# First pieces from the raw input, its squares in the second pass, zero matmuls ahead of the first product, another order of passes in each feed-forward and five early down tiles

## The chip, the cores and the metric

The kernel runs on one core of a Trainium2 chip, in one launch. The metric is the device time of that launch in microseconds (us). The engines are named as in the profile: PE (matrix products), PEld (its weight loads), DVE (vector), ACT (scalar), POOL (GpSimd) and SP (which here only issues DMAs). Each engine runs its instructions in the order of the program; they wait for each other and for DMAs on semaphores.

## The reference

A two-layer decoder trunk over 512 positions of width 2048, in float32. Each layer is a half feed-forward, a mixer and a half feed-forward, so there are four feed-forwards; only they and the last norm are touched by the change.

```python
def rms_norm(x, g):
    y = x32 * lax.rsqrt(jnp.mean(x32 * x32, axis=-1, keepdims=True) + NORM_EPS)
    return y * g

def swiglu(x, w_gate, w_up, w_down):
    return (jax.nn.silu(x @ w_gate) * (x @ w_up)) @ w_down      # 2048 -> 1536 -> 2048

for i in range(DEPTH):                                          # DEPTH = 2
    h = h + 0.5 * swiglu(rms_norm(h, norm_g[i, 0]), ffn_w_gate[i, 0], ffn_w_up[i, 0], ffn_w_down[i, 0])
    h = h + mixer(rms_norm(h, norm_g[i, 1]))                    # even_mixer or odd_mixer
    h = h + 0.5 * swiglu(rms_norm(h, norm_g[i, 2]), ffn_w_gate[i, 1], ffn_w_up[i, 1], ffn_w_down[i, 1])
return rms_norm(h, final_norm)
```

## The kernel before, in words

Activations lie transposed, 16 blocks of 128 channels by 512 positions. A product keeps float32 accuracy by splitting both factors into a high and a low part: `mm3` (lines 289 to 292) issues three matmuls, high by high, high by low, low by high.

**Weights.** `plan_and_uses` lists every weight tile in the order of use. SP loads them into nine `raw` buffers (line 246). `split_to` makes the high part `wh` on ACT (261) and the low part `wl` on DVE (262), and, for tiles that stand in `sums`, adds or subtracts two raw tiles on DVE (266). `take` keeps the splits seven tiles ahead of the one in use (`NSPL`): a split is issued in the engines' queues just before the matmuls of the tile seven ahead of it in use have their turn.

**A feed-forward's products.** Gate and up projections are formed by a scheme of seven products in place of eight, over halves of the input (`Pieces`: two input blocks give B11, B21, B22, T1 to T4). The 1536 hidden columns are three units of 512. For each unit `three` does three products (B11, B21, T4: 24 tiles, 144 matmuls, six PSUM banks) and `four` does four (T1, T3, T2, B22: 32 tiles, 192 matmuls, eight banks); a tile is 6 matmuls. The order is line 56:

```python
PASSES = ((0, 0), (1, 0), (0, 1), (2, 0), (1, 1), (2, 1))      # (unit, is it `four`)
```

B11, B21, B22 and T4 come from `Pieces.early` (486 to 500), T1 to T3 from `Pieces.late` (502 to 515), one pair of blocks at a time. Small work is laid between the tiles by generators: after each tile of `three`, `beside()` is called once and runs a generator to its next `yield`. In the first pass of the first feed-forward that generator is `first_pieces` (890 to 906): for each pair it scales the two input blocks by the gain on ACT (`xb`, 895), forms differences on DVE (490), splits (300, 301), and squares both blocks on ACT (372). In the second pass it is `then_late` (587 to 592): `late`, and after it the norm's reduction `ng`.

**The norm.** `Norm.add` (370 to 380) squares a block on ACT; from the third square on, GpSimd adds it with an accumulating DMA into one of two sums (378), and each such DMA waits on GpSimd for the one before it on the same sum. `Norm.stages` (382 to 392) reduces both sums over channels with 16 one-column matmuls on PE (`nps`, 387).

**After `four`.** `to_hidden` (548 to 577) forms the hidden unit: adds on DVE (549), two silus for each of two row halves on ACT (553, 557), four multiplications on DVE (565), then four times four transposes on PE (575) with a split each. It is a generator of 17 yields; the first transposes come at its 14th step. Unit 0's steps are run by the ticks of the fourth pass, the others in the last two `four` passes and among the down products.

**Down products.** The first `FIRST` = 4 output tiles keep a PSUM bank each (line 651) and are fed from the hidden units one after the other, 12 matmuls per tile and unit; the other tiles are done whole. In the last feed-forward `last` (1091 to 1100) scales the output blocks by the norm: of each eight pairs three on GpSimd, five on DVE.

Of the kernel before, what the change touches and what calls it, by code (L numbers as in the profile page):

```python
# [11 lines left out]
F32R = mybir.dt.float32r  # L12
# [37 lines left out]
NRAW = 9  # L50
NSPL = 7
# [4 lines left out]
PASSES = ((0, 0), (1, 0), (0, 1), (2, 0), (1, 1), (2, 1))  # L56

FIRST = 4
# [13 lines left out]
def plan_and_uses():  # L72
# [15 lines left out]
    def ffn_products(i, j, down):  # L88


        for u, four in PASSES:
# [26 lines left out]
    ffn_products(0, 0, PAIR_DOWN)  # L118
# [86 lines left out]
def trunk(ctx: ExitStack, tc: tile.TileContext, xT, pos_row, pos_col, wts, gains, consts, bias_a_in, bias_b_in, outT):  # L205
# [131 lines left out]
    nc.scalar.dma_start(gn, gains)  # L337
    for k in range(HK):
# [136 lines left out]
    class Pieces:  # L475
# [25 lines left out]

        def late(self):
# [19 lines left out]
    def ffn_products(pieces, norm, resid_in, sink, down, feed=None, beside=()):  # L522
# [25 lines left out]
        def to_hidden(u, c11, u2, s4, s5, s7, c12):  # L548
# [21 lines left out]
            yield  # L570
# [8 lines left out]
        def ahead_pieces():  # L579
            for k in range(HK):  # L580
                for e in range(k + 1, min(k + 4, HK)):
                    pieces.get(e, "B11", False)
                yield
                yield
                yield

        def then_late():
            for _ in range(HK):
                next(late, None)
                yield  # L590
                yield
            yield from ng
# [21 lines left out]
        def four(u):  # L614
# [3 lines left out]
            for k in range(HK):  # L618
# [3 lines left out]
                if k % 2:  # L622
                    tick()
# [6 lines left out]
                if k % 2:  # L630
                    tick()
# [3 lines left out]
            side.append(turned[u])  # L635

        feed = ahead_pieces() if feed is None else feed
        rest = then_late()
        for u, is_four in PASSES:
            if is_four:  # L640
                four(u)
            elif u == 0:
                three(u, lambda: next(feed, None))
                finish(feed)
            elif u == 1:
                three(u, lambda: next(rest, None))
                finish(rest)
# [10 lines left out]
        finish(turned[2])  # L658
        for pd, job in zip(pds, down):
            down_half(pd, job, hid, 4)  # L660
            down_done(pd, job, resid_in, sink)
# [227 lines left out]

    def first_pieces():  # L890
        for k in range(HK):
            bs = []
            for d in (k, HK + k):
                b = blk("xb")
                nc.scalar.activation(b, xs[d], AF.Copy, scale=g_norm(0)(d))
                bs.append(b)
            in0.add(k, *bs)
            del bs, b
            next(in0.work[k])
            yield  # L900
# [275 lines left out]
```

## Time and profile before

| | us |
|---|---|
| median of 3 timed runs | 2268.35 |
| lowest, highest | 2267.42, 2269.26 |
| the profiled execution, its time | 2269.59 |
| its span, first to last instruction | 2267.8 |
| PE busy in that span | 2218.3 |

The profiled execution's granted clock is 0.995 on average. About 1.8 us of its time lies outside the span. The page of the profile gives busy times, the span in 40 slices, the chain that ended last and the costliest groups of instructions; the trace behind it was asked for waits, stretches, single lines and instructions in order of time. A row `a <- b: t` of the waits reads: a stood idle t us until b was done.

### The profile page before, as it was taken

What the parts mean: (1) busy time and instruction counts of PE and PEld (TensorE: products, weight loads), DVE (VectorE), ACT (ScalarE), POOL (GpSimd) and SP (SyncE); (2) the same over time, 40 slices, a digit from 0 to 9 for tenths busy, and PEclk for the clock granted to TensorE, in tenths of its full rate; (3) what the DMA queues carried; (4) which work ended last, traced back from release to release, by engine and by line L of the source; (5) the groups of instructions that cost most, each with busy time, mean ns of one, the idle gap of its engine ahead of it and who ended that gap; (6) DMA issues with size and microseconds to landing.
All of it is one profiled execution on the core that took longest, in us unless ns stands there. A gap on an engine that the chain in (4) does not pass through costs nothing.

```text
span 2267.8 us, 30596 instructions
## 1 busy us (share of the span) xinstructions
PE 2218.3 (98%) x10272; PEld 1853.0 (82%) x10272; DVE 1570.6 (69%) x2694; ACT 1111.5 (49%) x2002; POOL 159.0 (7%) x190
## 2 busy tenths in 40 slices
PE   7999999999999999999999999999999999999997
PEld 5878788989888888878788878788888888878787
DVE  7979865464645578798646889855335677889734
ACT  8655444333334476555445554443235566554443
POOL 2000011000001020000010000011200010000013
PEclk9999999999999999999999999999999999999998
DMA  9756554423223396566577666554332377656444
GB/s 298 210 171 186 155 180 146 123 66 93 86 76 112 110 274 185 174 195 180 168 194 196 187 177 185 148 187 150 100 98 71 118 220 227 186 173 177 152 135 144
DMA packets 207981, 363.70 MB, mean 160 GB/s; under 512 B 23120, under 2 KB 46032, under 8 KB 207824
## 3 DMA queue, kind: packets, MB, share of 16 engines
q1 hardware_dynamic: 173552, 299.77, 44.6%
q10 hardware_dynamic: 26208, 47.30, 6.4%
q0 software_dynamic: 8064, 14.68, 3.8%
q8 instruction: 80, 1.31, 0.2%
q14 instruction: 77, 0.63, 0.1%
HBM read 321.82 MB, written 25.17 MB: 153 GB/s over the span
## 4 chain that ended last, share of the span: by engine, by line
PE 92%; DVE 3%; ACT 1%; issue 1%; DMA 0%; POOL 0%; DVEq 0%; ACTq 0%; POOLq 0%
PE pb L291 8%; PE pb L290 8%; PE pb L292 8%; PE pd L291 7%; PE pd L292 7%; PE pd L290 7%; PE pa L290 5%; PE pa L292 5%; PE pa L291 5%; PE pj L290 5%; PE pj L292 5%; PE pj L291 5%; PE wo L290 3%; PE wo L292 3%; PE wo L291 3%; PE pr L290 2%
## 5 line engine op out<-in xcount | busy, mean ns | idle before, releaser
L262 DVE TENSOR_TENSOR wl<-raw,wh 128x512 fp32r<-128x512 f32 (+3 forms) x1159 | 780.3, 686 | 465.2 <-ACT wh L261 442.4
L261 ACT ACTIVATE wh<-raw 128x512 fp32r<-128x512 f32 (+3 forms) x1159 | 689.6, 610 | 627.6 <-DVE wl L262 130.9
L290 PE MATMUL pd<-hidh,wh 128*128 128x512 f32 (+1 forms) x816 | 308.3, 378 | 2.9 <-ACT hidh L300 2.9
L291 PE MATMUL pd<-hidl,wh 128*128 128x512 f32 (+1 forms) x816 | 308.2, 378 | 1.4 <-DVE hidl L301 1.4
L292 PE MATMUL pd<-hidh,wl 128*128 128x512 f32 (+1 forms) x816 | 307.4, 377 | 0.0
L266 DVE TENSOR_TENSOR raw<-raw,raw 128x512 f32<-128x512 f32 x384 | 262.4, 683 | 0.0
L290 PE MATMUL pa<-wh,pbh 128*128 128x512 f32 x576 | 230.0, 399 | 16.0 <-ACT pbh L300 13.1
L291 PE MATMUL pa<-wl,pbh 128*128 128x512 f32 x576 | 227.6, 395 | 0.3
L292 PE MATMUL pa<-wh,pbl 128*128 128x512 f32 x576 | 227.5, 395 | 0.0
L290 PE MATMUL pj<-xgh,wh 128*128 128x512 f32 x464 | 181.7, 392 | 0.0
L292 PE MATMUL pj<-xgh,wl 128*128 128x512 f32 x464 | 180.8, 390 | 0.0
L291 PE MATMUL pj<-xgl,wh 128*128 128x512 f32 x464 | 180.7, 389 | 0.0
L290 PEld LDWEIGHTS pd<-hidh,wh 128*128 128x128 f32 x816 | 153.5, 188 | 31.7 <-ACT hidh L300 3.8
L291 PEld LDWEIGHTS pd<-hidl,wh 128*128 128x128 f32 x816 | 153.5, 188 | 31.5 <-DVE hidl L301 3.4
L292 PEld LDWEIGHTS pd<-hidh,wl 128*128 128x128 f32 x816 | 153.6, 188 | 27.6
L292 PE MATMUL pb<-wh,ptl 128*128 128x512 f32 x384 | 149.4, 389 | 0.0
L291 PE MATMUL pb<-wl,pth 128*128 128x512 f32 x384 | 149.4, 389 | 0.0
L290 PE MATMUL pb<-wh,pth 128*128 128x512 f32 x384 | 149.4, 389 | 0.0
L290 PEld LDWEIGHTS pa<-wh,pbh 128*128 128x128 f32 x576 | 110.2, 191 | 40.2 <-ACT pbh L300 14.8
L380 POOL TENSOR_TENSOR sq<-sq,sq 128x512 f32<-128x512 f32 (+1 forms) x50 | 61.8, 1237 | 1015.1 <-ACT sq L372 802.4
L292 PEld LDWEIGHTS pa<-wh,pbl 128*128 128x128 f32 x576 | 109.8, 191 | 25.0 <-DVE pbl L301 1.9
L291 PEld LDWEIGHTS pa<-wl,pbh 128*128 128x128 f32 x576 | 109.9, 191 | 24.1 <-DVE wl L262 2.0
(239 smaller groups left out, 3551.6 us busy)
## 6 DMA issues: line engine op xcount, KB each, us to landing
raw<-wts SPq DMA_DIRECT2D x1012, 256.0 KB, 2.9
spill<-x ACTq DMA_DIRECT2D x80, 256.0 KB, 3.0
x<-spill ACTq DMA_DIRECT2D x80, 256.0 KB, 3.0
raw<-wts SPq DMA_DIRECT2D x83, 192.0 KB, 2.4
sq<-sq POOLq DMA_DIRECT2D x56, 256.0 KB, 5.0
raw<-wts SPq DMA_DIRECT2D x48, 128.0 KB, 2.3
x<-xT SPq DMA_DIRECT2D x16, 256.0 KB, 5.4
x<-xT ACTq DMA_DIRECT2D x16, 256.0 KB, 3.4
```

What stands on the lines that cost most here:

```text
L261: nc.scalar.activation(h, src, AF.Copy)
L262: nc.vector.tensor_tensor(low, src, f32(h), op=ALU.subtract)
L266: nc.vector.tensor_tensor(to, a, b, op=ALU.add if sign > 0 else ALU.subtract)
L290: nc.tensor.matmul(out, ah, bh, start=start, stop=False)
L291: nc.tensor.matmul(out, ah, bl, start=False, stop=False)
L292: nc.tensor.matmul(out, al, bh, start=False, stop=stop)
L380: nc.gpsimd.tensor_tensor(acc, acc, sq, op=ALU.add)
```

## The change

- **First pieces.** `Pieces.from_raw` takes the place of scaling both blocks and calling `early`: ACT scales only the first block into `b1`; the second block's high part is made by ACT straight from the input with the gain, and DVE's differences take the gain with them. For the first pair, B11's half is split by itself, ahead of the differences.
- **Squares.** They leave the first pass. `first_squares` loads each input block a second time, by GpSimd's DMA queue, up to two blocks ahead, and squares it; `then_late` runs two of its steps after each step of `late`, so all 16 loads and squares lie in the second pass, and then finishes the norm's reduction.
- **Zeros.** Ten matmuls of a zero tile stand ahead of everything on PE.
- **Order of passes.** In feed-forwards two to four each unit's `four` follows its `three` at once; `late` and the norm's reduction move into the first pass (`pieces_beside`). The first feed-forward keeps the old order. `to_hidden` of a unit is now run by the ticks of the next `three` (and for what is left, four steps after each early down tile), and in `four` one step per pair; it has two more yields ahead of its transposes.
- **Early down tiles.** `FIRST` is 5.
- **Last scaling.** GpSimd helps only with the first half of the positions.

```diff
-PASSES = ((0, 0), (1, 0), (0, 1), (2, 0), (1, 1), (2, 1))
-FIRST = 4
+WARM = 10
+PASSES = ((0, 0), (0, 1), (1, 0), (1, 1), (2, 0), (2, 1))
+FIRST_PASSES = ((0, 0), (1, 0), (0, 1), (2, 0), (1, 1), (2, 1))
+FIRST = 5
...
+    idle, idle_ps = blk("idle", F32R), bank("idle")
+    nc.vector.memset(f32(idle), 0.0)
+    for _ in range(WARM):
+        nc.tensor.matmul(idle_ps, idle[:, :P], idle, start=True, stop=True)
...
+        def from_raw(self, k, x1, x2, g1, g2, apart):
+            t12, t3 = blk("t12"), blk("t3")
+            lo, hi = slice(0, H), slice(H, S)
+            sub = lambda o, a, b: nc.vector.tensor_tensor(o, a, b, op=ALU.subtract)
+            less = lambda o, b, c: nc.vector.scalar_tensor_tensor(o, b, g2, c, op0=ALU.mult, op1=ALU.subtract)
+            b1 = blk("xb")
+            h1, l1, h2, l2 = (blk("pb", F32R) for _ in range(4))
+            nc.scalar.activation(b1, x1, AF.Copy, scale=g1)
+            if apart:
+                nc.scalar.activation(h1[:, lo], b1[:, lo], AF.Copy)
+                sub(l1[:, lo], b1[:, lo], f32(h1[:, lo]))
+            nc.scalar.activation(h2, x2, AF.Copy, scale=g2)
+            less(l2, x2, f32(h2))
+            yield
+            sub(t12[:, lo], b1[:, hi], b1[:, lo])
+            less(t12[:, hi], x2[:, hi], t12[:, lo])
+            less(t3[:, lo], x2[:, hi], b1[:, hi])
+            less(b1[:, hi], x2[:, lo], t12[:, hi])
+            yield
+            c = hi if apart else slice(0, S)
+            nc.scalar.activation(h1[:, c], b1[:, c], AF.Copy)
+            sub(l1[:, c], b1[:, c], f32(h1[:, c]))
...
@@ to_hidden
-            yield
+            for _ in range(3):
+                yield
...
-        def ahead_pieces():
+        def pieces_beside():
             for k in range(HK):
                 for e in range(k + 1, min(k + 4, HK)):
                     pieces.get(e, "B11", False)
                 yield
+                next(late, None)
                 yield
+                if k > HK // 2:
+                    next(ng, None)
                 yield
 
         def then_late():
             for _ in range(HK):
                 next(late, None)
                 yield
-                yield
-            yield from ng
+                for _ in range(2):
+                    next(rest, None)
+                    yield
+            finish(rest)
+            finish(ng)
...
@@ four
-                if k % 2:
-                    tick()
+                for v in turned:
+                    next(turned[v])
...
+        made = [pieces_beside()] if feed is None else [feed, then_late()]
+        for u, is_four in passes:
             if is_four:
                 four(u)
+            elif made:
+                g = made.pop(0)
+                three(u, lambda: next(g, None))
+                finish(g)
             else:
+                before = min(turned)
+                side.append(turned[before])
                 three(u, tick)
-                finish(turned[0])
+                finish(turned.pop(before))
         pds = [bank("pd") for _ in range(FIRST)]
-        for u in range(2):
-            finish(turned[u])
+        for u in range(3):
+            for v in [v for v in turned if v <= u]:
+                finish(turned.pop(v))
             for pd, job in zip(pds, down):
                 down_half(pd, job, hid, UNIT // P)
-                tick(2)
+                if u == 2:
+                    down_done(pd, job, resid_in, sink)
+                    tick()
+                for _ in range(4 if u < 2 else 0):
+                    if turned and next(turned[min(turned)], 0) == 0:
+                        turned.pop(min(turned))
...
+    def first_squares():
+        got = {}
+        for d in range(NK):
+            for e in range(d, min(d + 3, NK)):
+                if e not in got:
+                    got[e] = blk("xn")
+                    nc.gpsimd.dma_start(got[e], xd[e])
+            norm0.add(got[d])
+            got[d] = None
+            yield
...
@@ last
-            eng = nc.gpsimd if (q // 2) % 3 == 1 else nc.vector
+            eng = nc.gpsimd if n == 0 and (q // 2) % 3 == 1 else nc.vector
```

## Rows read from the trace of the kernel before

**Rows 1.** The page's busy times, and the waits of PE: what waited, for what, us in total, times, longest.
```profile
PE 2218.3 (98%) x10272; PEld 1853.0 (82%) x10272; DVE 1570.6 (69%) x2694; ACT 1111.5 (49%) x2002; POOL 159.0 (7%) x190
...
PE ht L575 <- DVE s L565: 14.7, 18, 2.2
PE pa L290 <- ACT pbh L300: 13.1, 5, 8.9
PE pd L290 <- ACT hidh L300: 2.9, 4, 0.7
...
PE pd L291 <- DVE hidl L301: 1.4, 4, 0.3
```
**Rows 2.** Busy time by stretch: the stretch, its length, busy us of each engine (instructions), granted clock, DMA share, GB/s. The stretches are the first feed-forward's first two passes, then the second feed-forward's first three.
```profile
8.90:55.70 46.80, 39.63 (x145) 29.02 (x146) 38.09 (x71) 40.51 (x75) 11.39 (x13) 1.00 1.03 302
55.70:90.10 34.40, 34.40 (x161) 28.74 (x160) 29.72 (x54) 24.47 (x48) 2.28 (x2) 1.00 0.77 222
...
833.40:866.10 32.70, 32.70 (x146) 27.06 (x145) 22.37 (x39) 20.35 (x35) 2.33 (x3) 1.00 0.81 247
866.10:900.60 34.50, 34.50 (x162) 28.83 (x161) 28.69 (x51) 23.17 (x45) 1.43 (x1) 1.00 0.64 183
900.60:944.00 43.40, 43.40 (x193) 35.95 (x192) 37.22 (x59) 22.74 (x38) 0.00 (x0) 1.00 0.66 193
```
**Rows 3.** Instructions of the first pass in order of time (start, us, engine, line; idle before and what ended it), and the time to landing of the weight loads issued in the first 65 us (count, size, median us).
```profile
8.90 0.80 PE L290 MATMUL pa<-wh,pbh 128*128 128x512 f32 x1 [8.90 <-ACT pbh L300]
...
14.70 0.80 PE L290 MATMUL pa<-wh,pbh 128*128 128x512 f32 x1 [2.87 <-ACT wh L261]
...
16.50 23.18 SPq L246 DMA_DIRECT2D raw<-wts  x18
...
20.45 0.44 PE L290 MATMUL pa<-wh,pbh 128*128 128x512 f32 x1
...
51.11 0.50 PE L290 MATMUL pa<-wh,pbh 128*128 128x512 f32 x1 [1.15 <-ACT pbh L300]
...
55.62 0.39 PE L290 MATMUL pa<-wh,pbh 128*128 128x512 f32 x1
...
raw<-wts SPq DMA_DIRECT2D x44, 256.0 KB, 4.9
```
**Rows 4.** Groups of instructions of the first pass (8 to 56 us), shapes kept apart: count, busy us, mean ns of one, idle before.
```profile
L262 DVE TENSOR_TENSOR wl<-raw,wh 128x512 fp32r<-128x512 f32 x27 | 18.1, 686 | 4.8 <-ACT wh L261 4.6
...
L895 ACT ACTIVATE xb<-x,gn 128x512 f32<-128x512 f32 x14 | 9.2, 708 | 0.0
L300 ACT ACTIVATE pbh<-xb 128x512 fp32r<-128x512 f32 x16 | 9.2, 623 | 7.6 <-DVE xb L490 6.8 <-ACT wh L261 0.8
L372 ACT ACTIVATE sq<-x 128x512 f32<-128x512 f32 x16 | 9.1, 616 | 0.0
...
L490 DVE TENSOR_TENSOR t<-xb,t 128x256 f32<-128x256 f32 x7 | 2.9, 419 | 0.0
L539 ACT ACTIVATE s<-pa 128x512 f32<-128x512 f32 x2 | 1.1, 580 | 0.0
```
**Rows 5.** The accumulating DMAs of line 378: time from issue to landing in the stretches 0 to 65, 780 to 860 and 1100 to 1240 us, and one issue in order of time with its wait.
```profile
DMA to landing us min/median/max: 4.1/5.1/8.2
...
DMA to landing us min/median/max: 4.0/5.2/6.5
...
DMA to landing us min/median/max: 3.5/4.6/5.7
...
1880.19 0.86 POOL L378 DMA_DIRECT2D sq<-sq  x1 [2.68 <-DMA sq<-sq]
```
**Rows 6.** PE in order of time: the norm's reduction in the second pass.
```profile
78.74 1.84 PE L387 MATMUL nps<-ones,sq 128*128 128x1 f32 x16
```
**Rows 7.** PE in order of time at the first transposes of unit 0, second feed-forward (first three rows) and third (last row).
```profile
965.99 1.14 PE L575 MATMUL ht<-cs,s 128*128 128x128 f32 x3 [2.20 <-DVE s L565]
966.78 0.77 PE L290 MATMUL pa<-wh,pbh 128*128 128x512 f32 x1
...
969.47 0.60 PE L575 MATMUL ht<-cs,s 128*128 128x128 f32 x4
...
1339.95 0.44 PE L575 MATMUL ht<-cs,s 128*128 128x128 f32 x2 [1.33 <-DVE s L565]
```
**Rows 8.** DVE and ACT in order of time between the end of a `four` pass at 943.9 us and those transposes.
```profile
947.04 1.41 DVE L549 TENSOR_TENSOR s<-s,s 128x512 f32<-128x512 f32 x2
...
965.19 1.41 DVE L565 SCALAR_TENSOR_TENSOR s<-s,r,s 128x512 f32<-128x512 f32 x2
...
948.52 1.28 ACT L553 ACT_TABLE_LOAD   x1 [3.63 <-DVE s L549]
949.82 0.72 ACT L553 ACTIVATE s<-s,r 128x512 f32<-128x512 f32 x1
```
**Rows 9.** PE in order of time at the transposes among the second feed-forward's down products.
```profile
1082.72 0.44 PE L575 MATMUL ht<-cs,s 128*128 128x128 f32 x2 [1.12 <-DVE s L565]
1083.38 1.64 PE L575 MATMUL ht<-cs,s 128*128 128x128 f32 x13 [0.22 <-DVE s L565]
```
**Rows 10.** DVE in order of time: multiplications of the last scaling alone (first row) and beside GpSimd's (second).
```profile
2245.47 1.28 DVE L1099 TENSOR_TENSOR sc<-sc,R 128x512 f32<-128x512 f32 x2
...
2256.78 6.38 DVE L1099 TENSOR_TENSOR sc<-sc,R 128x512 f32<-128x512 f32 x5 [1.79 <-ACT R L399]
```

More of the change, by code (lines that the diff above doesn't have):

```diff
@@ L86, in cols, with ffn_products @@
         add(name, i, j, k0, k1, ((c0, c1),))
-    def ffn_products(i, j, down):
-        for u, four in PASSES:
+    def ffn_products(i, j, down, passes=PASSES):
+        for u, four in passes:
             c0, c1 = u * UNIT, (u + 1) * UNIT
@@ L116, in ffn_products @@
                 cols("ffn_w_down", i, j, 0, NF, d * P, d * P + P)
-    ffn_products(0, 0, PAIR_DOWN)
+    ffn_products(0, 0, PAIR_DOWN, FIRST_PASSES)
     for half in range(2):
@@ L337, in trunk @@
     nc.scalar.dma_start(gn, gains)
+    idle, idle_ps = blk("idle", F32R), bank("idle")
+    nc.vector.memset(f32(idle), 0.0)
+    for _ in range(WARM):
+        nc.tensor.matmul(idle_ps, idle[:, :P], idle, start=True, stop=True)
+    del idle, idle_ps
     for k in range(HK):
@@ L500, in early @@
             self.rest[k] = (t12, t3)
+        def from_raw(self, k, x1, x2, g1, g2, apart):
[20 more added lines that the diff above has]
+            sub(l1[:, c], b1[:, c], f32(h1[:, c]))
+            self.of[k] = {"B11": (h1[:, lo], l1[:, lo]), "T4": (h1[:, hi], l1[:, hi]), "B21": (h2[:, lo], l2[:, lo]),
+                          "B22": (h2[:, hi], l2[:, hi])}
+            self.rest[k] = (t12, t3)
+            self.work[k] = ()
         def late(self):
@@ L520, in get, with ffn_products @@
             return self.of[k].pop(name) if last else self.of[k][name]
-    def ffn_products(pieces, norm, resid_in, sink, down, feed=None, beside=()):
+    def ffn_products(pieces, norm, resid_in, sink, down, passes=PASSES, feed=None, rest=None, beside=()):
         hid = {}
@@ L888, in trunk @@
     u_diag, u_all = ur[:, 0:P], ur[:, P:2 * P]
+    xd = [xT[d * P:(d + 1) * P, :] for d in range(NK)]
     def first_pieces():
         for k in range(HK):
[L892 to L900, printed above, removed]
-            finish(in0.work[k])
-            yield
-            for d in (k, HK + k):
-                norm0.add(xs.pop(d))
+            yield from in0.from_raw(k, xs.pop(k), xs.pop(HK + k), g_norm(0)(k), g_norm(0)(HK + k), k == 0)
             yield
         nc.scalar.activation(ur, cs[:, 2 * P:4 * P], AF.Copy)
+    def first_squares():
[8 more added lines that the diff above has]
+            yield
     feed = first_pieces()
@@ L911, in trunk @@
         next(feed)
-    ffn_products(in0, norm0, reload([xT[d * P:(d + 1) * P, :] for d in range(NK)], PAIRS),
-                 make_sink(g_norm(1), norm1, xg1, spill0), PAIR_DOWN, feed, [rope_tables()])
+    ffn_products(in0, norm0, reload(xd, PAIRS), make_sink(g_norm(1), norm1, xg1, spill0), PAIR_DOWN, FIRST_PASSES, feed,
+                 first_squares(), [rope_tables()])
     xg, norm = xg1, norm1
```

16 lines of the change are left out of this document (removed).

## The prediction

> **What bounds the kernel now.** I read the page's busy times first: PE is busy 2218.3 of 2267.8 us [rows 1], so a change that removes no matmul can only win back the 49.5 us in which PE stands, or time in which it runs at the lower clock. Then the waits of PE, which say where that lies: 13.1 us on the first pieces (8.9 of it ahead of the first matmul), 2.9 on a weight split there, and 14.7 + 2.9 + 1.4 = 19.0 on the hidden units, in front of their transposes and of the products that read them [rows 1]. The rest is the tail after the last product. The stretches show that this is a matter of single places: the first pass of the first feed-forward takes 46.8 us with PE, DVE and ACT all at 81% or more, while the same pass in the second takes 32.7 [rows 2], which is 144 matmuls at 0.227. So a tile of 6 matmuls is 1.36 us and a pair of blocks (three tiles) 4.1.
>
> **First pass.** Before, ACT works per pair three weight splits, two scalings, two high parts and two squares: 3 x 0.62 + 2 x 0.71 + 2 x 0.62 + 2 x 0.62 = 5.8 us [rows 4], and from 22 us on the pass moves at that pace. One scaling and both squares go: 3.9 us, under PE's 4.1. DVE keeps its work: three low parts, two splits and four half-wide differences. In a row its full-wide operations follow each other at 0.6 (two in 1.28 where GpSimd is still [rows 10]) and the half-wide at about 0.4 [rows 4], so 5 x 0.6 + 4 x 0.4 = 4.6, with a short wait for ACT in between 4.7. DVE sets the new pace. What comes earlier in the pass decides less than it seems. Zeros and the split first half bring the first matmul to about 6.5 in place of 8.90, but the second tile waits for a split that stands behind the second pair's work on DVE, and the third pair's high part stands on ACT behind the split of the tenth tile. Its load is issued by SP at 16.50, after all of the input, and lands 4.9 us later [rows 3]; the change does not touch that order. So the seventh tile starts at 21.4 + 0.6 + 0.6 = 22.7 whatever the start was, against about 24.5 now (20.45 and three tiles). The last pair then starts at 22.7 + 5 x 4.7 = 46.2 and the pass ends at 50.3, with latencies 50.6, against 55.62 [rows 3]: **-5.0**. Bounds: at PE's own pace 47.2 (-8.4), at the old pace of 5.8 no gain (+0.2).
>
> **Squares in the second pass.** Now the norm's 16 small matmuls run at 78.74 without a wait [rows 6], because all squares are done in the first pass. After the change they stand directly behind the second pass's last product, and the squares are spread over that pass, two per pair. PE runs in order, so it stands until the last accumulation has landed. The accumulations on one sum follow each other at the landing time, since each waits on GpSimd for the one before [rows 5], and landings have a median of 5.2 us in the stretch with the nearest load (780 to 860). From the pass's start: ACT reaches the third square with the fifth tile, 4 x 1.36 + 0.6 = 6.1; the first accumulations go at 6.8 and 8.2; the 16th is the seventh on its sum and lands at 8.2 + 7 x 5.2 = 44.6, the pass ends at 32.7: PE stands **+11.9**. Lower bound: the last square is issued behind two copies that wait for the last product, so even with no queue it is 2 x 0.58 + 0.62 + the shortest landing, 3.5 [rows 4, 5]: 5.3. Upper bound: the longest landing of that stretch, 6.5, gives 53.7 and 21.0. The loads are on GpSimd's queue between the accumulations. No row has a plain load from GpSimd; with 0.9 to issue and a landing of 3.5 to 5 a load is back within the three steps (6.1) that it is ahead, so I cost it at nothing. Where it is late, ACT's queue stops at that square with the weight splits behind it; these are seven tiles, 9.5 us, ahead, and that is the cover. ACT itself is filled: 24.5 of 34.4 now [rows 2] plus 9.1.
>
> A page speaks differently here. The Trainium skill, DMA: Bandwidth & Descriptors, section Anatomy of one DMA — SWDGE (gpsimd) path, gives a DMA from GpSimd about 2.0 us and its bytes at 436 GB/s, by my estimate 2.6 us for 256 KB; by that the wait would be 4.4 and the sum about -8. No landing of rows 5 is under 3.5, and accumulations are what it counts here, so I hold to the rows.
>
> **The clock after that wait.** After 2.2 us of standing PE fell to the lower level: six matmuls took 2.69 us (966.78 to 969.47), 0.43 to 0.45 apart the spacing of the lower level (1.2 GHz), where 1.36 is usual [rows 7]; 1.3 lost. After the start's standing, twelve took 5.75 (14.70 to 20.45) in place of 2.72 [rows 3]; 3.0 lost, though the clock column of that stretch reads 1.00 [rows 2]. I take **+2.2** between these ends.
>
> **Hidden units.** Before: 19.0 us of waits, and three times (2.2 us gaps) the clock's 1.3, in all 22.9. At the transposes inside a `three` pass the rows are ready 2.2 us late [rows 7]; two more yields put them two tiles, 2.7 us, later. This wait goes, except for the last of four rows where a table load of 1.28 stands in the chain [rows 8]: three feed-forwards x 0.35 = 1.0. What is late next are the down products of feed-forwards two to four, where unit 2's whole chain now starts only when `four` ends. With that end as zero, the first two adds start at 3.1 (947.04 after 943.9) and take 1.41, a silu 0.72 [rows 8]. Two silus end at 6.0, the weight split behind them on ACT at 6.6, its low part on DVE at 7.2, the next two adds at 8.6, two silus at 10.1, again split and low part at 11.3, then four multiplications, two in 1.41 [rows 8]: 14.0. PE reaches the transposes after four down tiles, 4 x 12 x 0.227 = 10.9: 3.1 us late, against 2.65 now in the same place (1.12 + 0.22 [rows 9] and its share of the last two waits of rows 1). Three of these 9.3, and a fall of the clock in four of ten, 1.6. In the first feed-forward unit 1 has done eight of its steps by then and waits 0.7, unit 2 has seven down tiles of cover. After: 1.0 + 9.3 + 1.6 + 0.7 = 12.6, **-10.3**. Bounds: nothing left of the down waits (-21.2), or 3.1 and a clock fall each time with 2.2 still lost once per `three` (-4).
>
> **Fuller first passes.** In feed-forwards two to four `late` (8 x 1.0) and the following `four`'s first eight sums (8 x 0.6) come on top of DVE's 22.4 of 32.7 [rows 2]: 35.2, it ends 2.5 behind. The weights' lead covers that; the addition that frees the bank for the third product of `four` has 4.1 us of cover and takes 1.3. **+1.5** for three, between 0 and 3. The `four` pass behind it has DVE at 37.2 of 43.4 and wins it back. The order of passes moves no byte more, and the reduction comes 24 us into the pass, after the last accumulation has landed.
>
> **Tail.** Five multiplications beside GpSimd's take 6.38 us, alone they follow at 0.6 [rows 10]. Eight alone, the first one still disturbed: 5.3. **-1.1**, between 0 and -1.6.
>
> **Sum.** -5.0 + 11.9 + 2.2 - 10.3 + 1.5 - 1.1 = -0.8 against the profiled execution's 2269.6; that one lies 1.2 above the timed median of 2268.35, so 2267.6. A run of this kernel can tell 0.2%, 4.5 us, from no change.
>
> **Rivals.** (A) Accumulations land quickly. In the stretch with less traffic the shortest landing is 3.5 [rows 5]; then the chain (8.2 + 7 x 3.5 = 32.7) ends with the pass, only the bound of 5.3 is left and the clock loses 1.3: 7.5 less, 2260.1. For it: the first pass's accumulations no longer compete with it. Against it: the second pass then carries weights (222 GB/s now, [rows 2]), 16 loads and 14 accumulations. The Trainium skill's rule above would land here or a little lower. (B) Slower: the second pass runs into the DMA engines. At 302 GB/s they were busy to a share of 1.03 [rows 2], and landings reached 8.2. Weights at 194 (the 43.4 us stretch has 193), loads of two blocks and as many accumulations in each 4.1 us are 194 + 128 + 128 = 450 GB/s. If landings go to 6.5, PE stands 21.0: 9.1 more, 2276.7; from a mean landing of 6.0 on the kernel is slower than before by more than can be mistaken. The Trainium skill, same page, section Issuing engines are not separate DMA queues, says that DMAs of all issuing engines run on the same 16 engines and interleave, which is the same objection to a queue of their own for these loads. (C) The hidden chain is as short as its bare operations, and the down waits vanish with the clock falls: 10.9 less, 2256.7. For it: fewer weight splits lie among the down tiles. Against it: the splits stand behind the silus on ACT, as counted. (D) The zeros do not do what they say: the first tile runs faster, then PE stands again for the second. That changes nothing in the sum, which counts nothing for them.
>
> **How the numbers follow.** Forecast (within 4.5 us of 2268) 0.40, (A) 0.25, (C) 0.13, (B) 0.22. So faster 0.38, same 0.40, slower 0.22. The range takes in A and most of B and leaves out C and B's far end: 2257 to 2277.
>
> **What would show it.** In the changed profile: the first pass ends near 50.5, with small waits on the split pieces once per pair and DVE near full; PE stands some 12 us in front of the `nps` matmuls, waiting for an accumulating DMA, about 83 to 95, then runs matmuls 0.43 apart; the 2.2 us waits before transposes are gone; about 3 us of waits stand at the fourth early down tile of feed-forwards two to four, none such in the first; DVE alone ends the last scaling. The forecast is wrong if the wait before `nps` is under 7 or over 16 us, or if the down products run through.

## The result and the profile after

The changed kernel takes **2296.48 us** (median of 4 runs, 2295.61 to 2298.02) against 2268.81 for the kernel before in the same runs: ratio 1.0122, 95% interval 1.0104 to 1.0139. It is 27.7 us slower; the prediction, 2267.6 with a range from 2257 to 2277, was wrong. The profiled execution took 2298.0 with a span of 2296.2, 28.4 above the span before. The starts of the same products in both traces (between products and downs, the end of the last product) show where the time went:

| stretch | before, us | after, us | difference |
|---|---|---|---|
| start to the end of the first pass | 55.6 | 56.05 | +0.4 |
| second pass, `nps`, to the first `four` | 34.5 | 54.8 | +20.3 |
| first `four` | 43.5 | 46.2 | +2.7 |
| rest of feed-forward 1, its downs, to feed-forward 2 | 699.8 | 702.6 | +2.8 |
| products of feed-forward 2, then its downs | 237.2, 138.1 | 239.0, 136.5 | +0.2 |
| products of feed-forward 3, then downs and mixer | 234.6, 431.3 | 236.9, 429.4 | +0.4 |
| products of feed-forward 4, then all behind | 237.1, 156.1 | 241.5, 153.2 | +1.6 |

Busy time of the engines, and the waits of PE in the changed kernel (what waited, for what, us in total, times, longest), which answer to [rows 1]:

```profile
PE 2231.1 (97%) x10282; PEld 1862.8 (81%) x10282; DVE 1569.2 (68%) x2699; ACT 1110.8 (48%) x1995; POOL 182.1 (8%) x203
...
PE nps L396 <- DMA sq<-sq: 17.5, 2, 16.4
PE ht L613 <- DVE hidl L305: 11.2, 7, 2.2
PE ht L613 <- DVE s L602: 9.9, 13, 1.6
PE pa L294 <- ACT pb L532: 4.4, 5, 1.0
...
PE pb L294 <- DVE s L582: 0.9, 2, 0.5
```

The waits on the first pieces have shrunk, a wait of 17.5 us in front of the norm is new, and the hidden units wait 21.1 where 19.0 stood before; 11.2 of it for something that was not in the list, a low part `hidl`. PE is also 12.8 us longer busy: 4.6 of it are the ten matmuls of zeros, and it ran more of the others at the lower clock.

The stretches, as in [rows 2] (length; busy us of PE, PEld, DVE, ACT, POOL; granted clock; DMA share; GB/s): first pass, second pass, the norm, and the second `three` of feed-forward 2.

```profile
6.04:56.05 50.01, 39.91 (x146) 28.88 (x146) 42.63 (x78) 31.22 (x56) 2.96 (x5) 0.90 0.83 282
56.05:89.53 33.48, 32.99 (x145) 26.70 (x143) 20.58 (x36) 22.29 (x44) 12.42 (x18) 1.00 0.95 264
89.53:110.83 21.30, 3.75 (x17) 3.50 (x17) 10.65 (x18) 9.91 (x20) 5.90 (x8) 0.57 0.87 224
...
938.42:975.58 37.16, 35.24 (x161) 28.39 (x160) 31.68 (x53) 21.48 (x36) 0.00 (x0) 1.00 0.56 167
```

PE in order of time at the norm (start, us; idle before and what ended it), which answers to [rows 6]:

```profile
89.31 0.39 PE L296 MATMUL pa<-wh,pb 128*128 128x512 f32 x1
106.05 0.59 PE L396 MATMUL nps<-ones,sq 128*128 128x1 f32 x2 [16.36 <-DMA sq<-sq]
107.83 3.14 PE L396 MATMUL nps<-ones,sq 128*128 128x1 f32 x14 [1.19 <-DMA sq<-sq]
110.83 0.77 PE L294 MATMUL pb<-wh,pth 128*128 128x512 f32 x1
111.41 0.63 PE L295 MATMUL pb<-wl,pth 128*128 128x512 f32 x1
111.83 0.63 PE L296 MATMUL pb<-wh,ptl 128*128 128x512 f32 x1
```

Four costs follow: the waits of 16.36 and 1.19; the 16 small matmuls, 3.7 without that second wait where 1.84 stood, so 1.9 more; the first tiles of `four`, 0.43 apart, the lower level (1.2 GHz), which make up its 2.7; and 0.8 in the second pass itself, where PE waits once, 0.49, for a weight split.

### The profile page after: what moved, and what is told of

It reads as the page before. It is cut to its first block, busy times and chain, and to the rows that moved or that the text cites. A ratio compares the mean times of both kernels' runs of the same rounds, so it can differ in the third digit from the quotient of the medians.

```text
span 2296.2 us, 30652 instructions
## 1 busy us (share of the span) xinstructions
PE 2231.1 (97%) x10282; PEld 1862.8 (81%) x10282; DVE 1569.2 (68%) x2699; ACT 1110.8 (48%) x1995; POOL 182.1 (8%) x203
## 3 DMA queue, kind: packets, MB, share of 16 engines
q1 hardware_dynamic: 173552, 299.77, 43.7%
## 4 chain that ended last, share of the span: by engine, by line
PE 87%; DVE 5%; issue 3%; DMA 3%; ACT 1%; POOL 0%; DVEq 0%; POOLq 0%; SPq 0%; ACTq 0%
PE pd L294 8%; PE pd L295 8%; PE pd L296 8%; PE pb L294 7%; PE pb L295 7%; PE pb L296 7%; PE pj L294 5%; PE pj L296 5%; PE pj L295 5%; PE pa L294 3%; PE pa L295 3%; PE pa L296 3%; PE wo L294 3%; PE wo L295 3%; PE wo L296 3%
## 5 line engine op out<-in xcount | busy, mean ns | idle before, releaser
L294 PE MATMUL pa<-wh,pbh 128*128 128x512 f32 x432 | 171.4, 397 | 0.0
L295 PE MATMUL pa<-wl,pbh 128*128 128x512 f32 x432 | 169.0, 391 | 0.1
L296 PE MATMUL pa<-wh,pbl 128*128 128x512 f32 x432 | 169.1, 391 | 0.0
L387 POOL DMA_DIRECT2D sq<-sq x56 | 48.8, 871 | 744.0 <-ACT sq L381 397.0
L296 PEld LDWEIGHTS pj<-xgh,wl 128*128 128x128 f32 x464 | 87.1, 188 | 18.3
L295 PEld LDWEIGHTS pj<-xgl,wh 128*128 128x128 f32 x464 | 87.2, 188 | 17.4
```

The costliest lines, as they stand in the source:

```text
L294: nc.tensor.matmul(out, ah, bh, start=start, stop=False)
L295: nc.tensor.matmul(out, ah, bl, start=False, stop=False)
L296: nc.tensor.matmul(out, al, bh, start=False, stop=stop)
L387: nc.gpsimd.dma_start(acc, sq, accum_op=ALU.add)
```

## The experiments

Each ratio is against the kernel before in the same runs, with its 95% interval; the change itself stands at 1.0122.

### What the wait in front of the norm is made of

**a1_norm_late**: the reduction behind the first `four`.

```diff
             finish(rest)
-            finish(ng)
...
                 four(u)
+                finish(ng)
```

> The changed kernel with one edit: the norm's reduction is no longer finished behind the second pass's last product but behind the first `four`, so that PE has eight products per block to do before it needs the last accumulation. Theory 1 (the wait in front of `nps` is all of it: PE stands 17.5 us there, `nps` itself takes 4.6 us at the lower clock in place of 1.84, the tiles behind it lose 2.7): the accumulations land under 43 us of other work, and 20 to 24 us come back; about 2274. Theory 2 (ACT is what the late loads hold up: its squares wait 13.8 us for them, and the weight splits of the next pass stand behind those squares): the wait for an accumulation goes, but PE then waits for weight splits in the first `four`, and only about 10 us come back; about 2286.

Measured: 2281.05, ratio 1.0052 (1.0040 to 1.0065). The wait for an accumulation is gone, but the first `four` takes 53.7 us where it takes 43.7 in the kernel before: PE waits 4.4 us for ACT's copies of the pass before, which stand behind squares that wait for loads, then runs at the lower clock again. 15 come back, between the two theories; the cause is theory 2's, though PE waits for copies and hardly for weight splits (0.9).

**d2_tiles_kept**: the squares stay in the second pass, but from tiles kept since the first; no second loads.

```diff
-            yield from in0.from_raw(k, xs.pop(k), xs.pop(HK + k), g_norm(0)(k), g_norm(0)(HK + k), k == 0)
+            yield from in0.from_raw(k, xs[k], xs[HK + k], g_norm(0)(k), g_norm(0)(HK + k), k == 0)
...
-            norm0.add(got[d])
+            norm0.add(xs.pop(d))
```

> The changed kernel with the squares in the second pass, as there, but worked from the input's tiles that are kept from the first pass: nothing is loaded again. It has the prediction's chain of accumulations without the loads. Theory 1 (the loads, costed at nothing, are the difference: ACT waits 13.8 us for them, and they take part in filling the DMA engines): accumulations land in 3 to 4 us, ACT's squares wait for nothing, and PE waits 4 to 6 us in front of `nps`; about 2282. Theory 2 (the chain of accumulations sets the wait by itself, as the prediction had it, seven landings in a row at 5.2 or more): PE waits some 12 us; about 2290.

Measured: 2290.43, ratio 1.0096 (1.0081 to 1.0110). PE waits 12.5 us: theory 2, and near the 11.9 of the prediction. The trace has the issue and the landing of each accumulation. Here each from the third on, except the last, is issued 0.53 or 0.54 us after the one before it on its sum has landed, though its square has been ready for 1.2 to 5.8 us. So the chain sets the wait. It sets it in the change too: there the issue comes 0.53 to 0.58 us after the landing before it, and 1.2 to 2.6 us after the square, however long ACT has waited for the load. What the loads do is to slow the landings: the seven on the second sum take 39.9 us together in the change and 33.7 here, and that is the other 5 us. The end of the chain in the change:

```profile
101.97 0.63 ACT L381 ACTIVATE sq<-xn 128x512 f32<-128x512 f32 x1 [0.29 <-DVE s L582]
...
104.39 0.85 POOL L387 DMA_DIRECT2D sq<-sq  x1 [1.99 <-DMA sq<-sq]
```

The last square ends at 102.6, but its accumulation is issued at 104.39, when the one before it has landed (103.85).

**a5_gpsimd_sums**: `by_dma=True` removed from the first norm, loads kept.

> The changed kernel with the first norm's 14 sums worked by GpSimd (the same sums elsewhere in the kernel before took 1.29 us each) in place of accumulating DMAs; the loads of the tiles stay. Theory 1 (the chain of accumulations, each behind the one before at 5.6 us, is what PE waits for): without it the last sum ends some 1.3 us after the last square, the wait in front of `nps` falls from 17.5 to about 8, which is the lag of ACT alone (its last square ends 11.9 us after the pass's last product). Theory 2 (the loads are the bound: GpSimd has a load of 6 us on its queue, ACT's square waits for it, and only then the next one is asked for): the squares come just as late, and the wait falls by the last accumulation alone, about 3 us, to 14. By theory 1 about 2285, by theory 2 about 2293.

Measured: 2291.70, ratio 1.0098 (1.0085 to 1.0112); the wait is 12.1, between the two, and neither theory has its cause. The loads are no longer late (ACT waits 2.2 us for them in place of 13.8), but beside GpSimd's additions DVE is busy 31.6 us from 56.4 to 90.0 with 37 instructions, where it was 20.2 with 35: what was won on the DMA engines is lost on DVE. ACT then waits for DVE, the last square ends at 97.5, and GpSimd's last two additions, 6.74 us together, end at 102.1.

**a6_sp_loads**: `nc.sync.dma_start(got[e], xd[e])` in place of `nc.gpsimd`.

> The changed kernel with the 16 second loads issued by SP, on the queue of the weights, in place of GpSimd, where they stand between the accumulations. Theory 1 (order on GpSimd's queue: a load is asked for only when the accumulation in front of it has been let go): the loads come two or three tiles ahead of their squares, ACT's 13.8 us of waits for them go, and PE's wait in front of `nps` falls from 17.5 to about 10, the chain of accumulations with ACT's bound; about 2287. Theory 2 (the DMA engines, busy to 0.95 of that pass, are the bound): the loads land as late as now or the weights behind them do, and PE loses as much in another place; 2293 to 2297.

Measured: 2300.64, ratio 1.0140 (1.0126 to 1.0154): theory 2. PE's longest wait stays at 16.3, ACT waits longer for the loads (19.2), and the second pass grows from 33.6 to 40.6.

For three of these kernels, 56 to 112 us: ACT's wait for the loads, the DMA queues (packets, MB, share of 16 engines; GpSimd's is q0) and the median time to landing. First the change:

```profile
ACT sq L381 <- DMA xn<-xT: 13.8, 9, 2.9
...
q0 software_dynamic: 2896, 6.56, 53.1%
q1 hardware_dynamic: 3860, 7.02, 36.6%
...
sq<-sq POOLq DMA_DIRECT2D x14, 256.0 KB, 5.6
xn<-xT POOLq DMA_DIRECT2D x11, 256.0 KB, 6.5
```

Tiles kept (d2_tiles_kept), with PE's wait:

```profile
PE nps L396 <- DMA sq<-sq: 12.5, 2, 11.2
...
q1 hardware_dynamic: 4108, 7.46, 41.3%
q0 software_dynamic: 2016, 3.67, 40.0%
...
sq<-sq POOLq DMA_DIRECT2D x14, 256.0 KB, 4.4
```

Loads from SP (a6_sp_loads):

```profile
q1 hardware_dynamic: 6168, 11.22, 59.9%
q0 software_dynamic: 1847, 3.39, 34.2%
...
xn<-xT SPq DMA_DIRECT2D x16, 256.0 KB, 5.5
sq<-sq POOLq DMA_DIRECT2D x14, 256.0 KB, 6.1
```

These rows show that the engines fill: 53.1 + 36.6 = 90% of all 16 over these 56 us in the change, 94% with the loads on SP. They show too that 3.67 MB of accumulations take as much engine time (40.0%) as 7.46 MB of weights (41.3%). It is not the issuing engine alone: in a5_gpsimd_sums GpSimd's queue has loads only, and 2.88 MB take 19.3%. The Trainium skill, DMA: Bandwidth & Descriptors, section Issuing engines are not separate DMA queues, says that transfers of all issuing engines share the 16 engines; a6_sp_loads agrees: on SP's queue the loads keep ACT waiting for 19.2 us in place of 13.8, and the time is 2300.64.

### The first pass

**a2_squares_first**: squares in the first pass from the tiles that are there.

```diff
+            xa, xc = xs.pop(k), xs.pop(HK + k)
...
+            norm0.add(xa)
+            norm0.add(xc)
...
-                 first_squares(), [rope_tables()])
+                 iter(()), [rope_tables()])
```

> The changed kernel with one part undone: the squares are worked in the first pass from the tiles that are there, as before the change, and nothing is loaded again. The norm's wait must go in any case (17.5 us and about 5 of lower clock). Theory 1 (the first pass is a ring of short steps between ACT and DVE with a period of 5.63 us per pair, and neither engine is full): two squares of 0.62 on ACT lengthen ACT's part of the ring, by up to 1.2 us for each of 8 pairs; the first pass ends 5 to 10 us later, and the whole kernel is about 15 us faster than the change, about 2281. Theory 2 (the ring has slack on ACT, which waits 2.21 us per pair for DVE's last difference): the squares fit into that slack, the first pass ends where it ends now, about 56, and the kernel is about 23 us faster than the change, about 2273.

Measured: 2279.10, ratio 1.0045 (1.0032 to 1.0057). The first pass ends at 61.5, 5.5 later, and the time is 17 us under the change's: theory 1. Two squares of 0.62 that ACT could have worked in its idle time lengthen the pass. With the pieces built in this order the pass is worse than the old one, which had the squares and ended at 55.6.

**a3_pipelined**: the first step of pair k+1 ahead of the third of pair k.

```diff
-        for k in range(HK):
...
+        open_, left = {}, {}
+        for k in [0, 0, 0, 1, 1] + [e for k in range(1, HK - 1) for e in (k + 1, k, k + 1)] + [HK - 1]:
...
+            next(open_[k], None)
```

> The changed kernel with another order of issue in the first pass alone: the first step of pair k+1 (scaling, high and low part of the second block) is issued ahead of the third step of pair k (high part of the corrected first block), so that ACT has something to do while DVE works the four differences. Theory 1 (the ring of ACT and DVE sets the pace, 5.63 us per pair): the period falls towards the 4.6 to 4.7 us of DVE's own work, the first pass ends 5 to 7 us earlier, about 50; with the norm's wait unchanged behind it about 2290. Theory 2 (DVE's throughput beside GpSimd, or the arrival of input and weights, sets it): the period stays at 5.6 and the time within 2 us of the change, 2296.

Measured: 2295.09, ratio 1.0107 (1.0091 to 1.0122), by its time not told apart from the change; in the trace the first pass ends at 53.6, 2.4 earlier. The period falls as theory 1 has it, but the gain is half of its 5 to 7 us: the third pair starts only at 25.43, since ACT waits 4.99 us, until 22.48, for a weight load. ACT and DVE in the changed kernel, one period of the pass (start, us; idle before and what ended it):

```profile
39.60 0.63 ACT L532 ACTIVATE pb<-xb 128x512 fp32r<-128x512 f32 x1 [2.21 <-DVE xb L516]
...
45.24 0.63 ACT L532 ACTIVATE pb<-xb 128x512 fp32r<-128x512 f32 x1 [2.21 <-DVE xb L516]
...
36.38 0.75 DVE L516 SCALAR_TENSOR_TENSOR pb<-x,gn,pb 128x512 fp32r<-128x512 f32 x1 [0.46 <-ACT pb L523]
...
42.02 0.75 DVE L516 SCALAR_TENSOR_TENSOR pb<-x,gn,pb 128x512 fp32r<-128x512 f32 x1 [0.46 <-ACT pb L523]
```

and PE's waits in a3_pipelined:

```profile
40.90 0.50 PE L296 MATMUL pa<-wh,pb 128*128 128x512 f32 x1 [0.47 <-DVE pb L515]
45.74 0.50 PE L296 MATMUL pa<-wh,pb 128*128 128x512 f32 x1 [0.47 <-DVE pb L515]
```

In the change ACT waits 2.21 us for DVE's last difference and DVE then waits for ACT, in turns, 5.64 us a pair. With the other order the period is 45.74 - 40.90 = 4.84, and DVE has no gap from 33.45 to 46: it is DVE's own work. The 4.7 of the prediction is there, but not in the order of the change.

**a4_no_zeros**: the ten matmuls at the start removed.

> The changed kernel without the ten matmuls of zeros at the start. Theory 1 (they change nothing that lasts: the first tile runs faster behind them, but PE then stands 3.84 and 1.84 us for the second tile's weight split, and the next tiles run at the lower clock again): the first pass ends within 0.5 us of 56.05 and the time is that of the change, 2296. Theory 2 (the clock of the first tiles carries on to the pass's end): the first pass ends 2 to 3 us later, about 2299.

Measured: 2293.64, ratio 1.0107 (1.0093 to 1.0121), an interval that overlaps the change's; the first pass ends at 56.4, 0.4 later. Theory 1; the zeros are worth nothing that lasts.

### The hidden units

**b1_order_alone**: old pieces, squares and start; new order, two steps, five early tiles, tail.

```diff
-            yield from in0.from_raw(k, xs.pop(k), xs.pop(HK + k), g_norm(0)(k), g_norm(0)(HK + k), k == 0)
...
+            in0.add(k, *bs)
...
+                norm0.add(xs.pop(d))
```

> Pieces, squares and start of the kernel before, with the rest of the change: the order of passes in feed-forwards two to four, the two added steps ahead of the transposes, five early down tiles and the tail. By the comparison of the two traces, stage by stage: pass and downs of the first feed-forward +2.8, the second +0.2, the third +0.4, the fourth +2.9, the tail -1.3. Theory 1 (this part is a loss of its own, since the waits for hidden units only moved from behind the rows to the two free PSUM banks): 4 to 6 us slower than the kernel before, about 2273. Theory 2 (the stages differ by the clock's accidents and the order is neutral or a gain): 2265 to 2269.

Measured: 2272.45, ratio 1.0017 (1.0008 to 1.0025), 3.4 us slower by the medians: nearer to theory 1. So this half of the change, which was to win 9.9 (-10.3 + 1.5 - 1.1), loses, and the first feed-forward's half costs 2296.5 - 2272.5 = 24.

**b2_silu_apart**: additions and silus of `to_hidden` in steps of their own (four empty steps used up, none added).

```diff
                 add(s4[a], s4[a], s7[a])
-                nc.scalar.activation(s4[a], s4[a], AF.Silu, scale=norm.r[:, a:a + 1])
                 yield
+                nc.scalar.activation(s4[a], s4[a], AF.Silu, scale=norm.r[:, a:a + 1])
                 yield
                 add(s7[a], s7[a], s5[a])
-                nc.scalar.activation(s7[a], s7[a], AF.Silu, scale=norm.r[:, 2 + a:3 + a])
                 add(c12[a], c12[a], s5[a])
                 yield
+                nc.scalar.activation(s7[a], s7[a], AF.Silu, scale=norm.r[:, 2 + a:3 + a])
                 yield
```

> The changed kernel with one edit in the chain from sums to hidden units: each step's additions and its silu stand in steps of their own, so that DVE's next additions are issued a tile ahead of the silu that needs the last ones. Theory 1 (DVE and ACT wait for each other in turns, which makes a step of this chain 3.2 us long and the rows late): the 21.1 us that PE waits in front of transposes fall by half or more, about 2284. Theory 2 (the chain is as long as its operations and the weight splits between them; the same number of operations stands in front of the transposes): the waits stay within 3 us of 21.1, and the time within 4 of 2296.

Measured: 2274.34, ratio 1.0025 (1.0016 to 1.0034): 22 us back, more than theory 1. The waits for hidden units are 8.5 in place of 21.1. In the changed kernel, ACT, DVE and PE after the `four` that ends at 938.4:

```profile
944.18 0.72 ACT L590 ACTIVATE s<-s,r 128x512 f32<-128x512 f32 x1
...
947.38 0.72 ACT L594 ACTIVATE s<-s,r 128x512 f32<-128x512 f32 x1 [1.44 <-DVE s L586]
...
951.32 0.72 ACT L590 ACTIVATE s<-s,r 128x512 f32<-128x512 f32 x1 [2.17 <-DVE s L586]
...
945.45 1.29 DVE L266 TENSOR_TENSOR wl<-raw,wh 128x512 fp32r<-128x512 f32 x2 [2.65 <-ACT wh L265]
...
965.69 0.69 DVE L305 TENSOR_TENSOR hidl<-ht,hidh 128x512 fp32r<-128x512 f32 x1
...
966.43 0.66 PE L613 MATMUL ht<-cs,s 128*128 128x128 f32 x4 [1.86 <-DVE hidl L305]
```

The same place in b2_silu_apart, whose `four` ends at 933.4:

```profile
939.14 0.73 ACT L591 ACTIVATE s<-s,r 128x512 f32<-128x512 f32 x1
...
941.74 0.73 ACT L596 ACTIVATE s<-s,r 128x512 f32<-128x512 f32 x1 [0.84 <-DVE s L586]
...
945.07 0.72 ACT L591 ACTIVATE s<-s,r 128x512 f32<-128x512 f32 x1 [1.56 <-DVE s L586]
...
958.98 0.66 PE L613 MATMUL ht<-cs,s 128*128 128x128 f32 x4
```

A silu queued right behind its addition holds ACT for DVE (1.44, 2.17), the weight splits behind it wait, and DVE then waits for those (2.65, which holds a table load of 1.28 on ACT in both kernels; 2.05 in b2_silu_apart). With a step between, the first silus of the two row halves lie 5.93 apart in place of 7.14, and the third transposes run without a wait. The PSUM banks are as few as before, so it is DVE's lateness that made them too few.

**d1_six_steps**: `range(6)` for `range(3)` ahead of the transposes.

> The changed kernel with six, not three, empty steps ahead of the transposes of a unit's rows. Theory 1 (in a `three` pass the third transposes wait since the low part that frees a bank stands on DVE behind the weight splits that piled up during the chain; three tiles later that pile is worked off): the waits of 1.1 to 2.0 us at the third transposes and the clock behind them go, the `three` passes of feed-forwards two to four take 34.7 to 35 in place of 36 to 38.5, and of the first 35.5; the transposes among the early down tiles move most of a tile back, so that wait shrinks too; 10 to 20 us faster than the change, 2277 to 2287. Theory 2 (with six banks in use by the pass, two are too few wherever the transposes stand): the `three` passes stay at 36 to 38, only the down waits change; 2288 to 2296.

Measured: 2273.77, ratio 1.0026 (1.0017 to 1.0035), 22.7 back, though not where theory 1 had it. The waits among the down tiles are gone (9.9 to 0.2); at the third transposes they shrink only from 1.86 to 1.59 and from 1.1 to 0.6. DVE and PE there:

```profile
953.89 3.09 DVE L266 TENSOR_TENSOR wl<-raw,wh 128x512 fp32r<-128x512 f32 x5
956.90 0.68 DVE L270 TENSOR_TENSOR raw<-raw,raw 128x512 f32<-128x512 f32 x1
...
962.32 0.68 DVE L305 TENSOR_TENSOR hidl<-ht,hidh 128x512 fp32r<-128x512 f32 x1
...
963.05 0.66 PE L613 MATMUL ht<-cs,s 128*128 128x128 f32 x4 [1.59 <-DVE hidl L305]
```

DVE has no gap from 951.4 to 963: a low part and a sum for the next `four`, 1.2 us in each tile of 1.36, so three tiles later nearly the same pile stands in front of `hidl`. The backlog is the cause, as theory 1 said, but it does not wear off in three tiles.

**b3_three_steps**: three steps, not four, behind each early down tile.

```diff
-                for _ in range(4 if u < 2 else 0):
+                for _ in range(3 if u < 2 else 0):
```

> The changed kernel with three, not four, steps of the last unit's chain behind each early down tile, so that its transposes stand among the second round of those tiles and the chain has some 13 us of products in front of them in place of 10.9. Theory 1 (the waits in front of these transposes, about 2 us in each of feed-forwards two to four and more in the first, are the chain's lag behind PE): they go, with the clock's fall behind them, 6 to 9 us in all; about 2289. Theory 2 (the chain is slowed by the silus and weight splits in it, so that the wait only moves): within 2 us of 2296.

Measured: 2279.03, ratio 1.0046 (1.0033 to 1.0058), 17.5 back, twice what theory 1 had. The stretches behind the four feed-forwards' products shrink by 6.8, 4.3, 4.0 and 4.2. At feed-forward 2 in the change:

```profile
1110.31 0.33 PE L613 MATMUL ht<-cs,s 128*128 128x128 f32 x1 [0.84 <-DVE s L602]
1111.63 0.44 PE L613 MATMUL ht<-cs,s 128*128 128x128 f32 x2 [1.00 <-DVE s L602]
1112.30 0.33 PE L613 MATMUL ht<-cs,s 128*128 128x128 f32 x1 [0.22 <-DVE s L602]
```

2.06 of waits for 4.3 us: the other half is the lower clock behind them.

**c3_before_silu**: the silu edit alone on the kernel before.

> The kernel before with one edit, none of the change: additions and silus of the chain to the hidden units in steps of their own. It tells whether that edit needs the change's order of passes. Theory 1 (the two added steps and the order were needed as well, since the rows were 2.2 us late at the transposes of a `three` pass, which are two steps earlier here): the waits of 19.0 us fall by a part, 5 to 10; about 2260. Theory 2 (the turn-taking of ACT and DVE was the whole cause in the kernel before too): 15 to 20 us come back; about 2250.

Measured: 2240.18, ratio 0.9875 (0.9860 to 0.9890), 29.2 us faster than the kernel before. Theory 2 and beyond, and no new order was needed. Of the waits of 19.0 this is left:

```profile
PE ht L575 <- DVE s L565: 1.2, 6, 0.2
```

So 17.8 us of waits are gone; PE is also busy 2206.0 us in place of 2218.3 for the same 10272 matmuls, 12.3 less: the slower matmuls behind those waits are gone with them.

### Put together

**c1_order_silu** (b1_order_alone with the edits of b2_silu_apart and b3_three_steps):

> First pieces, squares and start of the kernel before, with the change's order of passes, five early down tiles and tail, and on top of them the additions and silus in steps of their own and three steps per early down tile. Theory 1 (the two edits act on the hidden units alone and do not depend on the first feed-forward's passes): the 22 us that the silu edit gave on the changed kernel come off the 2272.5 of the order alone, and 2 more from the steps; about 2248, faster than the kernel before. Theory 2 (part of those 22 us came from what the silu edit did in the first feed-forward or from the clock behind the long wait): 2255 to 2262.

Measured: 2239.03, ratio 0.9869 (0.9856 to 0.9883), better than theory 1. It is 1.15 under c3_before_silu, which the tail explains: order and early tiles are then worth nothing.

**c2_pieces_silu** (the change with a2, a3, b2 and b3 together):

> The changed kernel without the second loads: squares in the first pass from the tiles that are there, at the end of each pair's third step; the first step of pair k+1 issued ahead of the third of pair k; additions and silus in steps of their own; three steps per early down tile. The zeros stay. Theory 1 (the first pass is a ring that the order of issue opens, so that ACT has room for the squares): the first pass ends at 53 to 55 us, ahead of the 55.6 of the kernel before, and the whole takes 2 us less than the version with the old first pieces; about 2246. Theory 2 (with the squares ACT is full, or the input's arrival decides): the pass ends at 56 to 58; about 2249.

Measured: **2237.18**, ratio 0.9862 (0.9848 to 0.9875), 32 us faster than the kernel before and the fastest of all, though only 1.85 under c1_order_silu. Its first pass ends at 53.6, squares included, with a period of 4.84: theory 1, with ACT 26.4 and DVE 27.3 busy of the 30 us from 22 on. The gain over c1_order_silu is the 2 us that theory 1 names; that the whole is 9 us under its 2246 comes with the silu edit, as in c1_order_silu.

## Why the prediction was wrong, step by step

| step | predicted | measured |
|---|---|---|
| first pass | -5.0 | +0.4 |
| wait in front of `nps` | +11.9 | +17.5 |
| the second pass itself | 0 | +0.8 |
| the clock after it | +2.2 | +4.6 (1.9 in `nps`, 2.7 in `four`) |
| hidden units | -10.3 | +4.8 (what the other rows leave of 28.4) |
| fuller first passes | +1.5 | +1.6 |
| tail | -1.1 | -1.3 |
| sum | -0.8 | +28.4 |

**Hidden units**, the largest miss, 15 us, failed in "This wait goes". The rows did come in time; PE then stood at the third transposes. A `three` pass holds six of eight PSUM banks, and the third `ht` needs the first one emptied by `hidl`, which stands in DVE's pile (shown by b2 and d1). I asked only whether the rows were ready, and put 1.0 where the `three` passes, the first feed-forward's one with them, lost 14.7 against b2_silu_apart. In the downs 9.3 + 1.6 + 0.7 stands against 19.3 by b3: the waits of feed-forwards two to four were smaller than said (about 2.0 each for 3.1), the clock behind them, put at 1.6, cost about as much again as the waits (4.0 to 4.3 us in all for each), and the first feed-forward, put at 0.7, lost 6.8. And the gain to be had was larger than the 22.9 I counted: 29.2 by c3, because the slower matmuls behind the waits, which I counted at 3.9 of the 22.9, were worth about 12.

**Squares**: the chain was right in kind, in the change and in d2: each accumulation goes when the one before it on its sum has landed (in d2 all but the last). That 12.5 in d2 comes so near 11.9 is in part luck: the seven landings took 4.8 on average for my 5.2, and I had left out the 0.5 us between a landing and the next issue. The step that failed is "I cost it at nothing", of the loads. Their cost is not where I looked for it. ACT's squares did wait 13.8 us for them, but each square was ready before the landing that its accumulation waited for, and the cover that I named, seven tiles of weight splits, held but for 0.8 us. The loads cost their time on the DMA engines: the seven landings took 5.7 on average, and that is 5 us at PE. They themselves landed in 3.9 to 8.6, a median of 6.5 in the second pass, none near the 2.6 of my estimate; and five of the sixteen were issued in the first pass, between 18.55 and 35.62, not all in the second. This is rival (B), the DMA engines filling, with its price for the wait between forecast and rival; I gave it 0.22. It could be read from the trace before: I added bytes per second, where the queues of the first pass (8 to 56 us, kernel before) show that an accumulation takes twice the engine time of its bytes, 37.2% for 3.15 MB:

```profile
q1 hardware_dynamic: 6254, 11.38, 65.8%
q0 software_dynamic: 1728, 3.15, 37.2%
```

**First pass**: the step that failed is "DVE sets the new pace", 4.7 with "a short wait". DVE's work is 4.84, but a sum of busy times is a pace only if the order of issue lets the engine start; here ACT and DVE took turns at 5.64. The third pair also started at 24.3 for 22.7, behind the lower clock of the first tiles. The zeros, in (D), did what (D) said.

**The clock** was priced by one fall, between the 1.3 and the 3.0 read from the kernel before. The 2.7 in `four` lies between them; the step that failed is that the `nps` matmuls, which come first after the 17.5 us of standing, were left out, and they paid 1.9.

**Fuller first passes and tail** were right: two waits of 0.5 at the third product of `four`, and DVE alone with the last scaling, to be set against [rows 10]:

```profile
2286.55 5.00 DVE L1143 TENSOR_TENSOR sc<-sc,R 128x512 f32<-128x512 f32 x8 [1.78 <-ACT R L408]
```

What stays open: in the last `three` pass of feed-forward 4 the third transposes wait 2.03 us in the change, and the clock falls behind that wait; the pass takes 38.4 us. In a4_no_zeros and several other kernels of this study the same pass takes 35.8. Why that wait is sometimes longer is not shown. These 2.6 us are near the 2.8 by which the median of a4_no_zeros lies under the change's.

## What to carry to other kernels

Two in-order engines that hand a small chain back and forth are priced by the chain, not by their busy time: look for the instruction that is queued right behind what it waits for, and put other work between them, before moving anything larger. Where a wait is taken away, ask at once which buffer the next instruction of that engine needs and who empties it. Price DMAs by the engine time per byte that the queue rows show for their kind, not by bytes.

## What the runs showed of the hardware

An accumulating DMA cost the 16 engines about twice the time per byte of a weight load: 40.0% for 3.67 MB against 41.3% for 7.46 MB in d2_tiles_kept. In the change, three waits of 0.84, 1.00 and 0.22 us, all between 1109.4 and 1112.3, were followed by matmuls 0.43 apart, the lower clock, which about doubled the price of the waits in the downs. Behind a single wait of 1.07 (at 1045.77) or 1.86 (at 966.43) the matmuls stayed 0.23 apart; behind one of 2.03 (at 2088.52) they fell to 0.43. And beside GpSimd's additions DVE's 37 instructions took 31.6 us in a5_gpsimd_sums where 35 took 20.2 in the change.
